# One transformer block with a mixture of experts on one Trainium2 core: the second parts of the experts' weights move from two engines to one

## The chip, the core and the metric

The kernel runs as one program on one core of a Trainium2 chip. The core has a matrix engine (TensorE, PE in the profile; its weight loads are shown as PEld), a vector engine (VectorE, DVE), a scalar engine (ScalarE, ACT), a general-purpose engine (GpSimd, POOL) and a queue engine that issues most DMAs (SyncE, SP). Each engine runs its own list of instructions in order; an instruction waits on semaphores until what it needs is there. The metric is the device time of one execution, in microseconds; lower is better. Before the change it was 3081.26 us as the median of three runs, 3079.08 to 3086.68 us.

## The reference, cut to what matters

One layer of an encoder over 2048 tokens of width 1024: a mixer (differential attention beside a gated delta rule), then a mixture of experts. All inputs and outputs are float32. Only the last part matters here:

```python
def hier_moe(h, w_group, b_group, w_router, b_router, w1, w3, w2):
    ...                      # a token picks 1 of 4 groups, then 2 of the group's 8 experts
    def run(args):
        xblk, e = args       # a block of up to 128 tokens of expert e
        hid = jax.nn.silu(xblk @ w1[e]) * (xblk @ w3[e])
        return hid @ w2[e]
    yb = lax.map(run, (xb, blk_expert)).reshape(cap, D) * buf_w[:, None].astype(t.dtype)
    y = jnp.zeros((N, D), t.dtype).at[buf_tok].add(yb)
```

There are 32 experts; w1 and w3 are 1024 x 512 and w2 is 512 x 1024, so an expert has 6.3 MB of weights.

## The kernel before

The program has five phases, one after the other: the input projection, attention and the delta rule, the merge with the output projection, the routing, and the experts (`phase5`). The experts' stage is the last 900 us or so, and only it is touched.

**Two parts for every number.** PE multiplies in a shortened float format (fp32r). To keep float32's precision, a weight is split in two: a first part `hi`, a cast to the short format, and a second part `lo`, what the cast left out. A product x·w is made as three matmuls: x's first part with `hi` and with `lo`, and x's second part with `hi`.

**The work per expert.** `chunks` (L1546) loads an expert's weights as 12 tiles of 128 x 1024 float32, 512 KB each, on SP's queue, into a ring of 11 `raw` tiles (`NRAW`). `split` (L1561) takes the next loaded tile: ACT casts it to `hi` (L1568), another engine makes `lo` as raw minus hi (L1570), and SP issues one more load. `hi` and `lo` lie in rings of 12 tiles each (`NHI`, `NLO`), just one expert's worth; a tile of the next expert can be written only when the matmuls of the present one have read the tile in its place.

**Which engine makes `lo`.** `self.nsp` counts the splits. Of the first expert's twelve, numbers 2, 4 and 6 (`P0`) go to GpSimd, from the second expert on every fourth (`POOL`); the others go to DVE. That makes 96 on GpSimd and 288 on DVE. GpSimd also issues the gather of each block's tokens (L1579, L1637) and the scatter of its result (L1628, L1694) in this stage, in the same in-order list.

**A block.** The experts come in a fixed order by load rank (`ORDER`); an expert has one to three blocks, 46 in all: 34 full ones of 128 tokens (`block`, L1576) and 12 half ones of up to 64 (`half`, L1630). A full block gathers its tokens, transposes them on PE (`tx`, L1586), splits them (ACT `xh`, DVE `xl`, L1589), makes the products with w1 and w3 (`pa`, `pb`, L1597 and L1599: 48 matmuls), the gating (ACT L1605, DVE `hd` L1606 and L1607), a transpose and split of that (`th`, `dh`, `dl`), and the products with w2 (`py`, L1623 and L1624: 24 matmuls). A half block has 32 and 16 matmuls and a few more small DVE steps (`ha`, `hb`, L1667 to L1670). In an expert's last block, `split` is called between the matmuls, twelve times in all, for the next expert's tiles.

**What sets the order.** `pipeline` (L61) runs several blocks at once, each in a later step than the next. Within this, a scheduler in the framework places the instructions in each engine's list by its own estimate of when each will be ready, so a block's matmuls, another's transposes and a third's w2 products are interleaved on PE.

Of the kernel before, what the change touches and what calls it, by code (L numbers as in the profile page):

```python
# [9 lines left out]
F32 = mybir.dt.float32  # L10
# [4 lines left out]
ALU = mybir.AluOpType  # L15
# [21 lines left out]
NLO, NHI, NRAW, POOL = 12, 12, 11, 4  # L37
OHA, P0, KW, EB = (3,), (2, 4, 6), 7, 1
SPL = {0: 4, 2: 4, 3: 4}
NBLK = NEXP + N2 + N3  # L40
# [3 lines left out]
# gates of the last slab that wait for the attention, and the units of it that they come before  # L44
# [16 lines left out]
def pipeline(units, old_first=False):  # L61
    """each turn starts a unit and runs the older ones to their next "yield 1"; "yield 0" lets the others in between"""
# [19 lines left out]
class K:  # L82
# [59 lines left out]
    # ---------------------------------------------------------------- phase 1  # L142
    def phase1(self, late):
# [13 lines left out]
        with ExitStack() as ctx:  # L157
# [25 lines left out]
            def load_x(p):  # L183
                """two tiles of x, normalized"""
# [7 lines left out]
                # the second pair is waited for: its first tile by itself  # L192
# [100 lines left out]
            # per-partition gain of q: both maps' 64 channels  # L293
# [7 lines left out]
            # a head's scores are in units of its slope, a power of two, until the bias is on  # L301
# [254 lines left out]
    def gates_and_gdn(self, ctx, sm, ps, hxp, hh, hl):  # L556
# [33 lines left out]
        # softplus(x) = max(x, 0) + log1p(e), e = exp(-|x|); log1p(e) = ln(u) e / (u - 1), u = 1 + e  # L590
# [96 lines left out]
        def scan(t):  # L687
# [6 lines left out]
            for b in range(4):  # L694
                pb, o = slice(32 * b, 32 * b + 32), 32 * (b % 2)
                nc.sync.dma_start(T[pb, :, o:o + 32], TB[t, :, b].rearrange("h r c -> r h c"))
                nc.sync.dma_start(U[pb, :, o:o + 32], UB[t, :, b].rearrange("h r c -> r h c"))
                # the zero quarter of each pair of blocks
                G.memset((U if b % 2 else T)[pb, :, 32 - o:64 - o], 0.0)
# [11 lines left out]
            # inverse of the unit triangular matrix, block doubling 32 -> 64 -> 128  # L711
# [32 lines left out]
            # recurrence over tiles of 128 tokens  # L744
# [76 lines left out]
    # ---------------------------------------------------------------- branch merge  # L821
    def merge_setup(self, ctx, ps):
# [6 lines left out]
        def load_o(s, n, h):  # L829
            """a head's output of a slab, as parts"""  # L830
# [54 lines left out]
    # ---------------------------------------------------------------- phase 2  # L885
    def phase2(self, cm, late):
# [3 lines left out]
        with ExitStack() as ctx:  # L890
# [8 lines left out]
            # ---- constants  # L899
# [16 lines left out]
            # distances of keys from queries, the last chunk's first half of queries doesn't see its second half of keys  # L916
# [9 lines left out]
            # ---- attention  # L926
            kv, qs = {}, {}

            def kv_tiles(p, h, n):
                """the first 512 keys' tiles come last: their memory is free first"""  # L930
# [6 lines left out]
            def kv_load(p, h, n):  # L937
                """the keys and values of a head, n chunks"""
# [11 lines left out]
            def q_load(h, s):  # L950
# [7 lines left out]
                # numerators, their first maps' sums and sums of squares, of four query tiles  # L958
# [6 lines left out]
            def att(p, h, qt, sp_pool, w):  # L965
# [47 lines left out]
                # out = o / l1, rms-normalised; a mean square beyond float32 gives 0, as its rsqrt does  # L1013
# [27 lines left out]
            def units():  # L1041
# [14 lines left out]
                for i, (p, h, qt) in enumerate(todo):  # L1056
                    wn = TS * (p + 2)
                    if wn != w:
# [4 lines left out]
                        # the first pass's lies where the merge's tiles come, which are not to be loaded before  # L1063
# [31 lines left out]
    # ---------------------------------------------------------------- phase 3  # L1095
    def phase3(self, cm):
# [5 lines left out]
        with ExitStack() as ctx:  # L1102
# [72 lines left out]
            def outp(i, s, j):  # L1175
# [29 lines left out]
                # logits of a slab by columns: 36 rows of the weights' first parts, 36 of their second  # L1205
# [44 lines left out]
    # ---------------------------------------------------------------- phase 4  # L1250
    def route_consts(self, ctx):
# [3 lines left out]
        # descending weights 8..1, expert number, iota over slots columns and partitions  # L1255
# [14 lines left out]
        # an expert's share of the schedule, in half blocks: one, and one more for each of these its rank lies below  # L1270
# [3 lines left out]
        self.nsp = 0  # L1274
# [13 lines left out]
    def first(self, sm, x, n, tg):  # L1288
        """one-hot of the first maximum over the last axis of x, and the maximum"""
# [16 lines left out]
    def route_a(self, sm, t0, t1):  # L1306
        nc = self.nc
        V, A = nc.vector, nc.scalar
        n = t1 - t0
# [10 lines left out]
        # the two best experts of every group  # L1320
# [13 lines left out]
        # their weights  # L1334
# [10 lines left out]
    def route_b(self, c, sm, wk, wp, ps):  # L1345
# [8 lines left out]
        # loads of the experts, as a column and in every row  # L1354
# [6 lines left out]
        # positions of the assignments within their experts  # L1361
# [4 lines left out]
        # rank of an expert: experts in falling order of load, ties in expert order  # L1366
# [9 lines left out]
        # expert of a rank  # L1376
# [8 lines left out]
        # the schedule: NBLK blocks in rank order, what goes beyond an expert's share after them  # L1385
# [12 lines left out]
        # base, share and first further block of an expert in one number  # L1398
# [37 lines left out]
        # token and weight of a slot; the weight in two parts  # L1436
# [26 lines left out]
        # the other experts' weights are read after the first rows  # L1463
# [11 lines left out]
        # blocks beyond the schedule: how many, and each expert's range of them  # L1475
# [6 lines left out]
        def weights():  # L1482
# [5 lines left out]
            # halved, for the tanh form of silu  # L1488
# [5 lines left out]
    def spots(self, wk, wp, g, act=False):  # L1494
        """one-hot rows of the places in their blocks, of eight tiles of assignments"""
# [16 lines left out]
    def rows_of(self, pool, pt, nm):  # L1512
        """rows to gather and to add to, from a table of token numbers counted from 1, 0 where there is none"""
# [11 lines left out]
    # ---------------------------------------------------------------- phase 5  # L1525
    def phase5(self):
# [3 lines left out]
        with ExitStack() as ctx:  # L1530
# [15 lines left out]
            def chunks(e, i):  # L1546
                """loads of an expert's weights, two rows of 128 of w1 and w3 or one of w2 at a time"""
# [13 lines left out]
            def split(more):  # L1561
                """the next loaded weights' parts, and another load"""
# [236 lines left out]
```

## Time and profile before

| | |
|---|---|
| median of three runs | 3081.26 us |
| the profiled execution | span 3079.4 us from its first to its last instruction; the page lists no other time of it, and the median of the runs is 1.9 us above this span |
| mean granted TensorE clock | 0.966 |
| first DVE split, last result row scaled | 2171.1 us, 3066.3 us |
| PE's first matmul on a second part (`pa` of a half block) | 2180.6 us |
| DMA in the whole program | 561.20 MB |

A row of a grouped view reads: source line, engine, operation, what is written and read, shapes, count | busy us, mean ns of one | idle us of the engine before them, and who ended that idleness. A row of the timeline reads: start, length, engine, line, operation, how many were merged, and in brackets the idle time before it and its releaser. PE's matmuls overlap each other: one lasts 0.39 us, the next starts 0.23 us after it.

### The profile page before, as it was taken

Reading aid. Unit: us, or ns where it says so; the run is one execution under the profiler, and the core shown is the slowest. Engines: PE = TensorE matmul, PEld = TensorE weight load, DVE = VectorE, ACT = ScalarE, POOL = GpSimd, SP = SyncE. Lnnn points to the kernel's source line nnn. Section 1 sums busy time; section 2 is a strip of 40 time slices with the busy share of each in tenths; the row PEclk is TensorE's granted clock in tenths of the full one; section 3 lists DMA queues with packets and bytes.
Section 4 is the critical chain, followed back from the end, with each engine's and each line's share of the span. In section 5 each row is a group of like instructions: output and inputs, shape, how many; then the busy total and the mean of one; then the engine's idle time right before and its main releaser. Section 6 shows DMA issues by size and latency. Waiting matters only on the chain. (4 is left out here: it accounts for less than half of the span.)

```text
span 3079.4 us, 43963 instructions
## 1 busy us (share of the span) xinstructions
PE 2844.8 (92%) x14845; PEld 2294.6 (75%) x14845; DVE 2079.0 (68%) x4804; ACT 1332.7 (43%) x2409; POOL 837.8 (27%) x614
## 2 busy tenths in 40 slices
PE   6999999999999999999899999997799899999897
PEld 4888778777877777777788787786577677667675
DVE  7567669985276443377757655676867767886876
ACT  4512223333322333377555543221545545554554
POOL 2200000000221222001342324221544545543553
PEclk9999999999999999999999999998799999999998
DMA  6334652221554664585676647532978888886895
GB/s 224 119 86 117 202 182 80 79 67 53 165 144 130 185 179 147 149 200 148 167 179 171 168 110 235 195 144 103 324 240 259 260 258 292 294 291 217 271 312 148
DMA packets 426245, 561.20 MB, mean 182 GB/s; under 512 B 56520, under 2 KB 240920, under 8 KB 426016
## 3 DMA queue, kind: packets, MB, share of 16 engines
q1 hardware_dynamic: 340560, 440.87, 46.4%
q10 hardware_dynamic: 73744, 75.53, 7.3%
q0 software_dynamic: 11712, 41.95, 5.8%
q8 instruction: 119, 1.95, 0.3%
q14 instruction: 110, 0.90, 0.1%
HBM read 436.06 MB, written 122.18 MB: 181 GB/s over the span
## 5 line engine op out<-in xcount | busy, mean ns | idle before, releaser
L1570 DVE TENSOR_TENSOR low<-raww,hiw 128x1024 fp32r<-128x1024 f32 x288 | 434.4, 1554 | 46.8 <-ACT hiw L1568 44.2
L1568 ACT CAST hiw<-raww 128x1024 fp32r<-128x1024 f32 x384 | 378.8, 1048 | 153.6 <-PE py L1624 67.7
L1570 POOL TENSOR_TENSOR low<-raww,hiw 128x1024 fp32r<-128x1024 f32 x96 | 263.2, 2771 | 118.9 <-ACT hiw L1568 112.7
L982 DVE CUSTOM_DVE_ANT_0 sp<-sc,M 128x512 f32<-128x512 f32 (+1 forms) x320 | 183.6, 604 | 53.1 <-PE sc L980 52.0
L548 PE MATMUL pg<-hh,ghi 128*128 128x512 f32 x512 | 210.5, 411 | 2.5 <-ACT ghi L539 2.5
L332 PE MATMUL mma<-whi,hh 128*128 128x512 f32 x512 | 208.5, 407 | 2.4 <-ACT hh L248 1.0
L550 PE MATMUL pg<-hh,glo 128*128 128x512 f32 x512 | 208.3, 407 | 0.0
L549 PE MATMUL pg<-hl,ghi 128*128 128x512 f32 x512 | 208.0, 406 | 0.0
L334 PE MATMUL mma<-whi,hl 128*128 128x512 f32 x512 | 202.8, 396 | 0.6 <-DVE hl L249 0.6
L333 PE MATMUL mma<-wlo,hh 128*128 128x512 f32 x512 | 202.1, 395 | 0.4 <-DVE wlo L255 0.4
L987 ACT ACTIVATE sp<-sp,mx 128x128 f32<-128x128 f32 (+15 forms) x128 | 153.7, 1201 | 46.4 <-DVE mx L985 40.7
L1006 PEld LDWEIGHTS av<-V,aT 128*128 128x128 f32 x1088 | 140.2, 196 | 34.6 <-ACT aT L1004 26.7
L1006 PE MATMUL av<-V,aT 128*128 128x128 f32 x1088 | 151.6, 284 | 13.9 <-ACT aT L1004 12.7
L255 POOL TENSOR_TENSOR wlo<-raw,whi 128x512 fp32r<-128x512 f32 x12 | 16.9, 1428 | 533.0 <-ACT whi L254 533.0
L342 PE MATMUL mmb<-hh,whi 128*128 128x512 f32 x384 | 155.3, 404 | 5.4 <-ACT whi L254 5.4
L344 PE MATMUL mmb<-hh,wlo 128*128 128x512 f32 x384 | 151.1, 393 | 0.6 <-POOL wlo L255 0.4
L343 PE MATMUL mmb<-hl,whi 128*128 128x512 f32 x384 | 150.3, 391 | 0.0
L979 PE MATMUL sc<-K,qd 128*128 128x512 f32 (+1 forms) x320 | 132.1, 416 | 14.7 <-DVE mx L982 10.9
L1623 PE MATMUL py<-hiw,dh 128*128 128x512 f32 x272 | 115.1, 423 | 20.4 <-ACT dh L1614 20.3
L1597 PE MATMUL pb<-low,xh 128*128 128x512 f32 x272 | 112.7, 414 | 18.3 <-DVE low L1570 10.7
L1579 POOL DMA_INDIRECT x<-h,sgi x34 | 63.6, 1872 | 230.1 <-PE tx L1586 132.7
L1597 PE MATMUL pa<-low,xh 128*128 128x512 f32 x272 | 111.3, 409 | 11.9 <-DVE low L1570 11.9
(555 smaller groups left out, 7522.3 us busy)
## 6 DMA issues: line engine op xcount, KB each, us to landing
raww<-in_w_dram SPq DMA_DIRECT2D x384, 512.0 KB
mw<-in_w_ada_dram SPq DMA_DIRECT2D x64, 256.0 KB
gate<-gt ACTq DMA_DIRECT2D x64, 256.0 KB
g<-gate SPq DMA_DIRECT2D x64, 256.0 KB
graw<-in_w_in_dram SPq DMA_DIRECT2D x52, 256.0 KB
raw<-in_w_in_dram SPq DMA_DIRECT2D x22, 512.0 KB
K<-k_hi SPq DMA_DIRECT2D x36, 256.0 KB
K<-k_lo SPq DMA_DIRECT2D x36, 256.0 KB
```

The source lines that it names most:

```text
L332: nc.tensor.matmul(pt[:, :n], a, his[k][:, :n], start=(k == 0), stop=False)
L333: nc.tensor.matmul(pt[:, :n], a, los[k][:, :n], start=False, stop=False)
L334: nc.tensor.matmul(pt[:, :n], b, his[k][:, :n], start=False, stop=(k == KT - 1))
L342: nc.tensor.matmul(pt, a, hh[s][:, k, :], start=(k == 0), stop=False)
L548: nc.tensor.matmul(pt, hi[:, k, :], hh[:, k, :], start=(k == 0), stop=False)
L549: nc.tensor.matmul(pt, hi[:, k, :], hl[:, k, :], start=False, stop=False)
L550: nc.tensor.matmul(pt, lo[:, k, :], hh[:, k, :], start=False, stop=(k == KT - 1))
L982: V.tensor_tensor_reduce(out=b[:, k0:k0 + n], in0=pt[:, :n], in1=Mt[:, mo:mo + n], op0=ALU.add, op1=ALU.min, scale=SLOPES[h], scalar=3e38, ...
L1006: PE.matmul(av[:, :P], aT[:, k * P:(k + 1) * P], Vt[k4 // 4][:, k, :], start=(k4 + k == 0), stop=(k4 + k == qt))
L1568: A.copy(hi, raw)
L1570: on.tensor_tensor(out=lo, in0=raw, in1=hi.bitcast(F32), op=ALU.subtract)
L1597: PE.matmul(p_, xh[:, k, :], w[i, n, k][q], start=(k == 0 and q == 0), stop=False)
```

## The change

GpSimd no longer makes any second part; all 384 subtractions are on DVE. The two constants that chose the engine and the counter are gone. Comments are deleted all over the file as well, which moves the line numbers by 3 (L1570 of before is L1568 after, L1586 is L1583). The loads, the casts, the matmuls, the gathers and the scatters are the same in number and kind.

```diff
-NLO, NHI, NRAW, POOL = 12, 12, 11, 4
-OHA, P0, KW, EB = (3,), (2, 4, 6), 7, 1
+NLO, NHI, NRAW = 12, 12, 11
+OHA, KW, EB = (3,), 7, 1
...
-        self.nsp = 0
...
                 A.copy(hi, raw)
-                on = G if (self.nsp % POOL == POOL - 1 if i else self.nsp in P0) else V
-                on.tensor_tensor(out=lo, in0=raw, in1=hi.bitcast(F32), op=ALU.subtract)
-                self.nsp += 1
+                V.tensor_tensor(out=lo, in0=raw, in1=hi.bitcast(F32), op=ALU.subtract)
```

The scheduler makes new lists out of this. Three places follow; in a tile's name the first number is the expert's place in the order, the second the tile's own.

GpSimd's list early in the stage, before the change:

```order
L1570 TENSOR_TENSOR low_2_21691<-raww_2_21558,hiw_2_21690 128x1024
L1579 DMA x_21993<-h_18355,sgi 128x1024
L1570 TENSOR_TENSOR low_2_21827<-raww_2_21606,hiw_2_21826 128x1024
L1628 DMA out_dram<-yo_21780,ssi 2176x1024
L1570 TENSOR_TENSOR low_3_21899<-raww_3_21664,hiw_3_21898 128x1024
L1570 TENSOR_TENSOR low_3_21939<-raww_3_21803,hiw_3_21938 128x1024
L1637 DMA x_22181<-h_18355,sgi 64x1024
```

The same place after the change:

```order
L1576 DMA x_21993<-h_18355,sgi 128x1024
L1625 DMA out_dram<-yo_21780,ssi 2176x1024
L1634 DMA x_22181<-h_18355,sgi 64x1024
L1625 DMA out_dram<-yo_21963,ssi 2176x1024
L1576 DMA x_22316<-h_18355,sgi 128x1024
```

What moved: the four subtractions between the gathers and the scatters are gone from this list, and nothing stands in their place.

DVE's list where the tiles of the fourth expert in the order (`low_3`) are made, before the change; `ha`, `hb` and `xl` below are steps of a half block and of the block behind it:

```order
L1627 SCALAR_TENSOR_TENSOR yo_21780<-py_21795,wt,g_21029 128x512
L1589 TENSOR_TENSOR xl_21837<-tx_21845,xh_21836 128x512
L1570 TENSOR_TENSOR low_3_21863<-raww_3_21622,hiw_3_21862 128x1024
L1570 TENSOR_TENSOR low_3_21869<-raww_3_21640,hiw_3_21868 128x1024
L1570 TENSOR_TENSOR low_3_21893<-raww_3_21646,hiw_3_21892 128x1024
L1570 TENSOR_TENSOR low_3_21913<-raww_3_21670,hiw_3_21912 128x1024
L1570 TENSOR_TENSOR low_3_21919<-raww_3_21688,hiw_3_21918 128x1024
L1570 TENSOR_TENSOR low_3_21933<-raww_3_21694,hiw_3_21932 128x1024
L1667 TENSOR_TENSOR ha_21944<-ha_21944,pa_21852 64x512
L1667 TENSOR_TENSOR hb_21945<-hb_21945,pb_21853 64x512
L1589 TENSOR_TENSOR xl_21996<-tx_21997,xh_21995 128x512
```

The same place after the change, with one more row ahead of it:

```order
L1568 TENSOR_TENSOR low_2_21827<-raww_2_21606,hiw_2_21826 128x1024
L1624 SCALAR_TENSOR_TENSOR yo_21780<-py_21795,wt,g_21029 128x512
L1586 TENSOR_TENSOR xl_21837<-tx_21845,xh_21836 128x512
L1568 TENSOR_TENSOR low_3_21863<-raww_3_21622,hiw_3_21862 128x1024
L1568 TENSOR_TENSOR low_3_21869<-raww_3_21640,hiw_3_21868 128x1024
L1568 TENSOR_TENSOR low_3_21893<-raww_3_21646,hiw_3_21892 128x1024
L1568 TENSOR_TENSOR low_3_21899<-raww_3_21664,hiw_3_21898 128x1024
L1568 TENSOR_TENSOR low_3_21913<-raww_3_21670,hiw_3_21912 128x1024
L1568 TENSOR_TENSOR low_3_21919<-raww_3_21688,hiw_3_21918 128x1024
L1568 TENSOR_TENSOR low_3_21933<-raww_3_21694,hiw_3_21932 128x1024
L1568 TENSOR_TENSOR low_3_21939<-raww_3_21803,hiw_3_21938 128x1024
L1664 TENSOR_TENSOR ha_21944<-ha_21944,pa_21852 64x512
```

What moved: eight subtractions stand in a row ahead of `ha`, `hb` and `xl` where there were six, and one more (`low_2_21827`) stands ahead of the `yo` before them; the three are GpSimd's of the first fence.

PE's list at the second transposes of that same block (`tx_22004`, which write into a PSUM tile that `xl_21996` has to read first), before the change:

```order
L1597 MATMUL pa_22011<-low_3_21893,xh_21836 128x512
L1586 MATMUL tx_22004<-ident,x_21834 128x128 x4
L1597 MATMUL pb_22012<-hiw_3_21898,xh_21836 128x512
L1623 MATMUL py_21964<-hiw_2_21799,dh_21959 128x512
L1623 MATMUL py_21964<-low_2_21800,dh_21959 128x512
```

After the change, the end of the matmuls that now come first, with the same transposes behind them:

```order
L1594 MATMUL pb_22012<-hiw_3_21918,xh_21836 128x512
L1594 MATMUL pb_22012<-low_3_21919,xh_21836 128x512
L1596 MATMUL pa_22011<-hiw_3_21912,xl_21837 128x512
L1583 MATMUL tx_22004<-ident,x_21834 128x128 x4
L1620 MATMUL py_21964<-hiw_2_21799,dh_21959 128x512
L1620 MATMUL py_21964<-low_2_21800,dh_21959 128x512
```

What moved: between `pa` with `low_3_21893` and the transposes stand 15 matmuls of 128x512 that stood behind them before. In a like place of the sixth expert in the order, nine matmuls now stand ahead of the first `py` that stood behind its first four; elsewhere the two lists agree over long stretches.

## The prediction

> **What bounds the kernel now.** I read the page's engine totals first, then its costliest groups, then the windows of the experts' stage, then who PE waits for, and last the timeline at PE's longest stops. The two lists of the changed engines' work on the page:
>
> ```profile
> span 3079.4 us, 43963 instructions
> ...
> L1570 DVE TENSOR_TENSOR low<-raww,hiw 128x1024 fp32r<-128x1024 f32 x288 | 434.4, 1554 | 46.8 <-ACT hiw L1568 44.2
> ...
> L1570 POOL TENSOR_TENSOR low<-raww,hiw 128x1024 fp32r<-128x1024 f32 x96 | 263.2, 2771 | 118.9 <-ACT hiw L1568 112.7
> ```
>
> The reader sees 288 subtractions on DVE at a mean of 1554 ns and 96 on GpSimd at 2771 ns. The windows view of the stage, from PE's settled start to the last block's end (busy us of PE, PEld, DVE, ACT, POOL; granted clock; DMA share; GB/s):
>
> ```profile
> 2203.00:3067.00 864.00, 796.92 (x3512) 610.96 (x3511) 647.96 (x636) 466.29 (x587) 425.84 (x179) 0.96 0.81 264
> ```
>
> PE is busy 797 of 864 us, DVE 648: PE bounds the stage, and 67 us of it are PE's own idle time. The 0.96 is a second loss: 4% of 864 us, or 35 us, went in a slower clock. Who ended PE's idle time, in total us, times and longest, from the waits of PE from 2200 us on:
>
> ```profile
> PE py L1623 <- ACT dh L1614: 20.3, 9, 5.3
> PE tx L1586 <- DVE xl L1589: 15.5, 3, 5.2
> PE pa L1597 <- DVE low L1570: 11.9, 13, 2.2
> PE pb L1597 <- DVE low L1570: 10.7, 11, 2.6
> PE pb L1597 <- POOL low L1570: 7.6, 6, 5.0
> ```
>
> These five rows are 66 us, nearly all of it. Only the last names GpSimd; why the others matter to this change is in the single durations of one DVE subtraction (min/median/max ns), and of `yo`'s last step in half blocks, with that step's group:
>
> ```profile
> L1570 DVE TENSOR_TENSOR low<-raww,hiw x288: 1203/1214/5653, 2171.1 to 3051.8; 128x1024 fp32r<-128x1024 f32 x144
> L1692 DVE SCALAR_TENSOR_TENSOR yo<-yo,wt,g x24: 733/744/2966, 2211.1 to 3050.0; 64x512 f32<-64x512 f32 x24
> ...
> L1692 DVE SCALAR_TENSOR_TENSOR yo<-yo,wt,g 64x512 f32<-64x512 f32 x24 | 36.8, 1535 | 0.2
> ```
>
> Most take 1.21 us, a few up to 5.65. Against the medians DVE loses 288 x (1554 - 1214) = 98 us and 24 x (1535 - 744) = 19 us, together **117 us**. Where it goes shows at PE's longest kind of stop (DVE, then POOL, then PE, in the timeline):
>
> ```profile
> 2240.46 12.82 DVE L1570 TENSOR_TENSOR low<-raww,hiw 128x1024 fp32r<-128x1024 f32 x6
> 2254.41 0.67 DVE L1589 TENSOR_TENSOR xl<-tx,xh 128x512 fp32r<-128x512 f32 x1
> ...
> 2243.59 2.99 POOL L1570 TENSOR_TENSOR low<-raww,hiw 128x1024 fp32r<-128x1024 f32 x1
> 2246.76 3.17 POOL L1570 TENSOR_TENSOR low<-raww,hiw 128x1024 fp32r<-128x1024 f32 x1 [0.18 <-ACT hiw L1568]
> ...
> 2255.14 1.11 PE L1586 MATMUL tx<-ident,x 128*128 128x128 f32 x4 [5.19 <-DVE xl L1589]
> ```
>
> Six subtractions take 12.82 us on DVE while GpSimd makes two. Six undisturbed ones are this long (and PE stops briefly there too):
>
> ```profile
> 2356.57 6.88 DVE L1570 TENSOR_TENSOR low<-raww,hiw 128x1024 fp32r<-128x1024 f32 x6
> ...
> 2362.38 0.50 PE L1597 MATMUL pb<-low,xh 128*128 128x512 f32 x1 [0.40 <-DVE low L1570]
> ```
>
> So in a row one takes 6.88 / 6 = 1.15 us, and DVE lost 5.9 us to two subtractions of GpSimd, about their whole length: the two engines hardly make `lo` at once. DVE then reaches `ha`, `hb` and `xl` late, and PE waits.
>
> **The change part by part.** *Removed:* 96 subtractions on GpSimd, and with them DVE's 117 us. *Added:* 96 x 1.15 = 110 us on DVE. DVE's sum is therefore the same within 7 us, some 640 of 864 us; the gain is not less work but where it falls. I go by kinds of stop.
>
> *`xl`.* At 2240 us two parts come to DVE (2.3 us), and one more ahead of `yo` (1.15): 5.9 - 3.4 = 2.5 us of the 5.19 go, 48%; of 15.5 us, **7.5**.
>
> *`dh`.* The usual place, DVE and PE:
>
> ```profile
> 2318.13 7.49 DVE L1570 TENSOR_TENSOR low<-raww,hiw 128x1024 fp32r<-128x1024 f32 x3 [0.30 <-ACT hiw L1568]
> ...
> 2327.40 0.79 PE L1623 MATMUL py<-hiw,dh 128*128 128x512 f32 x1 [3.54 <-ACT dh L1614]
> ```
>
> Three subtractions lose 7.49 - 3.4 = 4.1 us; two parts come to DVE (2.3); 1.8 of 3.54 us go, half; of 20.3 us, **10.3**.
>
> *`low` behind DVE.* One of three like places:
>
> ```profile
> 2734.24 13.24 DVE L1570 TENSOR_TENSOR low<-raww,hiw 128x1024 fp32r<-128x1024 f32 x6
> ...
> 2743.10 0.50 PE L1597 MATMUL pa<-low,xh 128*128 128x512 f32 x1 [1.00 <-DVE low L1570]
> ...
> 2746.40 0.79 PE L1597 MATMUL pb<-low,xh 128*128 128x512 f32 x1 [2.57 <-DVE low L1570]
> ```
>
> Here 13.24 - 6.9 = 6.3 us are lost to three parts that cost 3.4 on DVE: 2.9 of the 3.57 us go, 81%. Of the 22.6 us I take out about 4 that belong to late loads (below), so **14** to 15; I take 14.
>
> *`low` behind GpSimd.* 7.6 us, 5.0 in one stop. A part on DVE takes 1.2 us instead of 2.8 and never stands behind a scatter: **5**.
>
> *Clock.* 35 us. The next two rows are a stop of 2.2 us and the stretch just after it:
>
> ```profile
> 2586.70:2589.00 2.30, 0.09 (x2) 0.06 (x1) 2.30 (x3) 1.04 (x1) 0.00 (x0) 1.00 1.10 310
> 2589.26:2592.67 3.41, 3.25 (x8) 2.11 (x7) 3.41 (x5) 2.26 (x4) 2.52 (x1) 0.50 1.05 329
> ```
>
> The clock was halved for 3.4 us after a stop of only 2.2. The stops above shrink to 2.7, 1.7 and 0.7 us, so many remain long enough. The ends are 0 and 35; I take a third, **11**.
>
> *Against it.* In bursts without collisions, as at 2356 us, GpSimd's two parts ran for free and DVE now has 2.3 us more ahead of a stop that exists already. I find three such bursts, and five with one part: between 0 (DVE idles there later) and 13 us; I take **8**, nearer the upper end because PE already waits there.
>
> *Scatters and gathers* stay on GpSimd with nothing between them. GpSimd's own waits for gathers are for a free buffer:
>
> ```profile
> POOL x L1579 <- PE tx L1586: 132.7, 20, 12.5
> ...
> PEld tx L1644 <- DMA x<-h,sgi: 7.7, 1, 7.7
> ```
>
> A gather is thus issued as soon as PE has read an older block's tokens, and PE waits for one only once, the stage's first; they cost nothing, and would only if their lead over PE were gone. *SP, ACT:* the loads and casts keep their order; a `raw` tile is free sooner, which can only help the loads.
>
> Sum: 7.5 + 10.3 + 14 + 5 + 11 - 8 = **40 us**. The profiled span is 3079.4 us and the median 1.9 above it, so 3081.3 - 40 = **3041 us**.
>
> **The rivals.**
>
> *Zero sum.* 117 us go, 110 come; if the wait only moves along DVE's list, the time stays within 9 us (0.3%, about what a measurement of this kernel tells from no change): 3081 less the 7 us of the sums, 3074. For it: DVE's list is in order and `xl`, `hd` and `yo` now stand behind more subtractions. Against: DVE has 216 idle us in the stage.
>
> *Loads.* The stage moves 864 us x 264 GB/s = 228 MB. The fastest long stretch, and casts that wait for a load:
>
> ```profile
> 2592.00:2660.00 68.00, 65.56 (x296) 50.80 (x295) 51.70 (x53) 39.36 (x48) 35.06 (x17) 1.00 0.95 331
> ...
> 2585.51 1.05 ACT L1568 CAST hiw<-raww 128x1024 fp32r<-128x1024 f32 x1 [1.82 <-DMA raww<-in_w_dram]
> ...
> ACT hiw L1568 <- DMA raww<-in_w_dram: 8.4, 8, 2.4
> ```
>
> At 331 GB/s the 228 MB need 689 us, so the whole is not bound by them; but where experts of one block follow each other the share is already 0.95, and PE can't go faster there. If half of the gain falls in such stretches, 20 us are left: 3061.
>
> *A better plan.* PE's new list has 15 matmuls (15 x 0.234 = 3.5 us) ahead of the `tx` that waits, more than the 2.7 us that I left, and nine (2.1 us) ahead of a `py` against 1.8. If that holds throughout, the rest of `xl` and `dh` (18 us) and half of the clock (12) go too: 70 us, 3011.
>
> *The clock comes back whole.* If the shortened stops no longer halve the clock, the term is 35 instead of 11: 3017. For it: the two windows are one pair, and the 5.19 and 3.54 us stops are the common ones. Against it: in that pair 2.2 us were enough. The Trainium skill, "TensorE: Matmul & The Clock Gate", section "What's actually happening", says that the clock falls to half after an idle window of about 3.4 us, which would be this rival; the quoted pair speaks against the rule.
>
> *Slower.* DVE becomes the bound in last blocks: twelve parts are 13.8 us, beside 4 to 6 us of a block's own steps, against 12 us of matmuls in a half block. If only the bursts at PE's some 15 longer stops count as lost time (5.4 us each, the mean of the three quoted, 81 us) but all 110 added us are in PE's way, the time grows by 29 us to 3110. It decides by whether DVE's idle time lies in the blocks that get the parts. The Trainium skill, "Perfetto Trace Analysis", section "Optimizing Scalar/DVE Operations", says that where DVE is saturated, moving work to GpSimd may make sense, though it might not help since the two share a read port: undoing that would cost time if DVE were full. At 648 of 864 us the trace does not show it full.
>
> **How the numbers follow.** Chances: forecast 0.38 (3041, some 15 either way), loads 0.16 (3061), a better plan 0.13 (3011), the clock 0.05 (3017), zero sum 0.12 (3074), slower 0.16 (3110). The first four are faster by over 0.3%: 0.72; the same 0.12; slower 0.16. The range takes in the clock's case, the better plan (2999 with all of the clock, which I cut to 3002), the zero sum, and the milder half of the slower case, up to 3092; about 0.15 is left outside.
>
> **What would show it.** In the changed kernel's profile: 384 DVE subtractions with mean near the 1214 ns median and no maximum above 1.5 us; no `low` on POOL; DVE busy near 640 us in the stage; PE's waits for `dh` and `xl` halved, for POOL `low` gone; a mean clock in the stage near 0.97. Wrong would be: DVE subtractions still over 1.5 us on average (the loss was not GpSimd's); PE waiting as long in total but for DVE `low` (zero sum or slower); or `hiw` waiting for loads by tens of us.

## The result: 2996 us, and where PE's stops went

The changed kernel takes 2996.28 us (median of four runs, 2989.41 to 3000.1), the kernel before 3083.97 us beside it (3079.08 to 3087.09): 0.9719 of its time, with a 95% interval of 0.9703 to 0.9734, or some 87 us less. The direction was forecast, the size wasn't: 3041 us, and 3002 at the low end of the range.

All of it lies in the experts' stage. Its start can be read off the last matmuls ahead of it, `ptab`; first the kernel before, then the changed one (the operation's durations, then its first and last start, from a tile's view):

```profile
L1460 PE MATMUL ptab<-oc,oh x32: 376/387/407, 2161.8 to 2170.0; 128*128 128x46 f32 x32
```

```profile
span 2997.3 us, 43960 instructions
...
L1459 PE MATMUL ptab<-oc,oh x32: 377/387/405, 2164.4 to 2172.7; 128*128 128x46 f32 x32
```

From there to the end of the span it was 3079.4 - 2161.8 = 917.6 us, and is 2997.3 - 2164.4 = 832.9: **85 us less**. What lies ahead of it is the same work. Its length scatters: among the runs below `ptab` starts between 2148 and 2164 us where nothing ahead of it was changed, so stages are compared, not the ends of two profiles.

The groups of the page and a tile's view show DVE without collisions:

```profile
L1568 DVE TENSOR_TENSOR low<-raww,hiw 128x1024 fp32r<-128x1024 f32 x384 | 445.9, 1215 | 21.3 <-ACT hiw L1567 20.6
```

```profile
L1568 DVE TENSOR_TENSOR low<-raww,hiw x384: 1204/1215/1232, 2173.7 to 2969.4; 128x1024 fp32r<-128x1024 f32 x192
```

The mean is the median, and the longest of 384 took 1.23 us where it had been 5.65. DVE's sum is 446 us in place of 434: as forecast, the gain isn't less work for DVE. The windows view of the stage (busy us of PE, PEld, DVE, ACT, POOL; clock; DMA share; GB/s) and PE's waits in it:

```profile
2205.00:2985.00 780.00, 762.06 (x3497) 590.19 (x3495) 639.13 (x729) 462.46 (x585) 164.26 (x88) 1.00 0.89 292
```

```profile
PE py L1620 <- ACT dh L1611: 10.1, 9, 1.8
PE pa L1594 <- DVE low L1568: 4.9, 5, 3.6
PE py L1621 <- DVE dl L1612: 1.2, 1, 1.2
PE tx L1583 <- DVE xl L1586: 0.8, 1, 0.8
PE pb L1594 <- DVE low L1568: 0.4, 1, 0.4
```

PE's idle time went from 67 us to 18, its waits from 66 to 17, and the clock from 0.96 to 1.00. Its busy time fell from 797 to 762 us on the same matmuls but for 15 that the window doesn't show (some 3.5 us), since fewer of them ran at half clock. DMA carries 292 GB/s at a share of 0.89, and ACT's casts wait 0.7 us for a load in the whole stage: the loads were not the limit.

One long stop is left. The timeline shows DVE, then PE:

```profile
2428.07 8.02 DVE L1568 TENSOR_TENSOR low<-raww,hiw 128x1024 fp32r<-128x1024 f32 x7
...
2433.88 0.50 PE L1594 MATMUL pa<-low,xh 128*128 128x512 f32 x1 [3.61 <-DVE low L1568]
```

DVE's row counts the parts that start before the view's end at 2435 us. PE goes on at 2433.88 us, 5.81 us after the row's start: that is about five parts of 1.15 us, so it needs the row's fifth part and simply arrives before it is made, behind the small steps that end a half block.

### The profile page after: what moved, and what is told of

Its sections match the earlier page's. It is cut to its first block, busy times and chain, and to the rows that moved or that the text cites. A ratio compares the mean times of both kernels' runs of the same rounds, so it can differ in the third digit from the quotient of the medians.

```text
span 2997.3 us, 43960 instructions
## 1 busy us (share of the span) xinstructions
PE 2815.3 (94%) x14845; PEld 2276.4 (76%) x14845; DVE 2068.7 (69%) x4900; ACT 1331.4 (44%) x2409; POOL 567.2 (19%) x518
## 3 DMA queue, kind: packets, MB, share of 16 engines
q8 instruction: 119, 1.95, 0.3%
## 5 line engine op out<-in xcount | busy, mean ns | idle before, releaser
L1568 DVE TENSOR_TENSOR low<-raww,hiw 128x1024 fp32r<-128x1024 f32 x384 | 445.9, 1215 | 21.3 <-ACT hiw L1567 20.6
L1006 PEld LDWEIGHTS av<-V,aT 128*128 128x128 f32 x1088 | 138.9, 194 | 33.6 <-ACT aT L1004 25.5
L1576 POOL DMA_INDIRECT x<-h,sgi x34 | 73.1, 2150 | 360.9 <-PE tx L1583 204.0
L980 PE MATMUL sc<-K,ql 128*128 128x512 f32 (+1 forms) x320 | 119.6, 381 | 2.0 <-DMA ql<-q_lo 2.0
L1620 PE MATMUL py<-hiw,dh 128*128 128x512 f32 x272 | 109.9, 404 | 10.3 <-ACT dh L1611 10.1
L332 PEld LDWEIGHTS mma<-whi,hh 128*128 128x128 f32 x512 | 97.0, 189 | 25.2 <-ACT hh L248 1.7
L334 PEld LDWEIGHTS mma<-whi,hl 128*128 128x128 f32 x512 | 96.9, 189 | 23.0 <-DVE hl L249 1.7
```

Of the source, the lines that this page charges most:

```text
L332: nc.tensor.matmul(pt[:, :n], a, his[k][:, :n], start=(k == 0), stop=False)
L334: nc.tensor.matmul(pt[:, :n], b, his[k][:, :n], start=False, stop=(k == KT - 1))
L1006: PE.matmul(av[:, :P], aT[:, k * P:(k + 1) * P], Vt[k4 // 4][:, k, :], start=(k4 + k == 0), stop=(k4 + k == qt))
L1568: V.tensor_tensor(out=lo, in0=raw, in1=hi.bitcast(F32), op=ALU.subtract)
```

## The experiments

Three explanations were open: the end of the collisions between DVE and GpSimd (theory C); the new order of PE's list, which the scheduler made (rival O); and DVE's time as such, its own or stretched (theory D). In the diffs below, `hold_pe(ORDER)` stands for a few lines that tie each of PE's instructions of the stage, by a table, behind its predecessor in the list named; it adds no wait for data. The diffs also leave out the setting up of counters and scratch tiles. Holding a list costs nothing by itself: in the run stops (below), which holds the changed kernel's own list, 819.0 us lie between the first `ptab` and the last `yo` of a full block, in the changed kernel 819.5 us.

| run | what | us | of the kernel before | 95% interval |
|---|---|---|---|---|
| oldorder | changed kernel, PE's list of before | 3034.2 | 0.9837 | 0.9821 to 0.9853 |
| neworder | kernel before, PE's list of the changed one | 3084.4 | 1.0004 | 0.9990 to 1.0019 |
| pool2 | changed, useless subtractions on GpSimd | 3123.3 | 1.0132 | 1.0116 to 1.0149 |
| dve2 | changed, the same on DVE | 3085.9 | 1.0005 | 0.9990 to 1.0021 |
| dve2_free | dve2, PE's list not held | 3068.4 | 0.9970 | 0.9952 to 0.9987 |
| dve1 | half of dve2's | 3034.8 | 0.9861 | 0.9835 to 0.9886 |
| pool1 | changed, useless copies on GpSimd | 3008.5 | 0.9769 | 0.9739 to 0.9799 |
| dose48 | kernel before, 48 parts on GpSimd for 96 | 3026.5 | 0.9838 | 0.9817 to 0.9860 |
| slackorder | changed, PE's list of dve2_free | 2995.1 | 0.9740 | 0.9717 to 0.9764 |
| tx_old | changed, second transposes as early as before | 3014.7 | 0.9797 | 0.9778 to 0.9816 |
| tx_new | oldorder, second transposes as late as after | 3038.0 | 0.9885 | 0.9863 to 0.9906 |
| after_again | changed kernel | 2988.7 | 0.9726 | 0.9708 to 0.9744 |
| merge_dve, merge_dve5 | changed, the merge's parts on DVE too | 2984.9, 2980.9 | 0.9684, 0.9684 | 0.9656 to 0.9712, 0.9663 to 0.9704 |

Differences in us below are differences of these ratios times 3084, unless they are of stages.

### PE's list against the collisions

oldorder keeps all parts on DVE and takes PE's order from before:

```diff
             pipeline(units())
+            hold_pe(ORDER_OF_BEFORE)
```

> All 384 subtractions on DVE as after the change, but PE's list in the experts' stage is held to that of before the change, instruction by instruction. Theory C (the end of the collisions between DVE and GpSimd is the whole gain, PE's list matters little): within 10 us of the changed kernel's 2996, so 2990 to 3006. Rival O (PE's new list, with more matmuls ahead of those that wait, made the stops shrink beyond my forecast): the stops that I had left for xl and dh come back, 18 us, and half of the clock's loss, 14 us or so: 3020 to 3035, with PE's waits for dh and xl at 25 us or more.

It took 3034 us, at the upper end of rival O's range, with PE's waits for `dh` and `xl` at 22 us where O expected 25. The move to DVE alone, with PE's list as it was, is worth 0.0163, or **50 us** (43 by the stage, below); the new list is worth 0.0118, **36 us** more. PE's waits and the stage in this run:

```profile
span 3032.9 us, 43970 instructions
...
L1532 PE MATMUL ptab<-oc,oh x32: 376/387/406, 2158.6 to 2166.9; 128*128 128x46 f32 x32
```

```profile
2200.00:3020.00 820.00, 777.51 (x3505) 596.37 (x3505) 638.65 (x726) 464.94 (x586) 163.37 (x87) 0.99 0.84 277
```

```profile
PE py L1693 <- ACT dh L1684: 14.2, 9, 2.8
PE tx L1656 <- DVE xl L1659: 8.0, 3, 2.7
PE pa L1667 <- DVE low L1641: 7.2, 6, 1.9
PE py L1694 <- DVE dl L1685: 4.8, 8, 0.9
PE py L1756 <- DVE dh L1748: 2.4, 9, 0.4
PE tx L1656 <- DVE dh L1748: 2.0, 1, 2.0
PE pb L1667 <- DVE low L1641: 2.0, 5, 0.4
```

The stage is 3032.9 - 2158.6 = 874.3 us. From before to oldorder PE's idle time fell by 67.1 - 42.5 = 24.6 us and its busy time by 19.4; from oldorder to the changed kernel by 24.5 and 15.4. So both steps are half stops and half clock (the windows differ by seven and eight matmuls, some 2 us each).

The place that the prediction worked through shows both steps. Before, PE stopped there for 5.19 us. In oldorder, DVE and PE:

```profile
2235.98 9.16 DVE L1641 TENSOR_TENSOR low<-raww,hiw 128x1024 fp32r<-128x1024 f32 x8
2246.25 0.68 DVE L1659 TENSOR_TENSOR xl<-tx,xh 128x512 fp32r<-128x512 f32 x1
...
2246.99 0.66 PE L1656 MATMUL tx<-ident,x 128*128 128x128 f32 x4 [2.71 <-DVE xl L1659]
```

In the changed kernel:

```profile
2238.93 9.16 DVE L1568 TENSOR_TENSOR low<-raww,hiw 128x1024 fp32r<-128x1024 f32 x8
2249.21 0.68 DVE L1586 TENSOR_TENSOR xl<-tx,xh 128x512 fp32r<-128x512 f32 x1
...
2250.61 0.60 PE L1583 MATMUL tx<-ident,x 128*128 128x128 f32 x4
```

DVE does the same in both, eight parts in 9.16 us and then `xl`. In oldorder PE stands for 2.71 us; in the changed kernel no bracket stands behind the transposes: other matmuls come first, and `xl` is done when PE gets there.

neworder is the converse, the kernel before with PE's new list:

```diff
             pipeline(units())
+            hold_pe(ORDER_OF_AFTER)
```

> The subtractions on both engines as before the change (96 on GpSimd), but PE's list is held to that of the changed kernel. Theory C: as before the change within 15 us, 3069 to 3099, DVE's subtractions still at a mean of about 1.55 us. Rival O: PE's better list hides a good part even with the collisions, 3030 to 3055.

3084 us, no change: theory C's figure. The new list is worth nothing while GpSimd still makes parts:

```profile
PE pb L1670 <- POOL low L1643: 25.5, 13, 3.1
PE pa L1670 <- DVE low L1643: 17.9, 9, 4.8
```

PE now waits 25.5 us for GpSimd's parts, where it was 7.6: it comes to them at a place that fits a DVE part. So the two gains aren't independent; the list's 36 us need GpSimd's parts gone.

The two lists differ more than the three places shown ahead of the prediction tell: of PE's 3609 instructions that the tables hold, 460 have to be moved to make one list of the other, and the second group of transposes stands elsewhere in 32 of the 46 blocks. To see which part of the list counts, the second group of a block's transposes was put back to its old distance behind the first in the new list (tx_old), and to its new distance in the old list (tx_new). Counted in the lists with 0.23 us for a matmul, the mean distance over the 46 blocks is 5.6 us of work before and 7.0 after.

```diff
             pipeline(units())
+            hold_pe(ORDER_OF_AFTER, second_tx_as_in=ORDER_OF_BEFORE)
```

> The changed kernel with its own PE list, except that the second group of a block's transposes stands as early behind the first as before the change (counted in PE instructions between them; 32 of 46 blocks differ). Theory X (the later place of instructions that wait for DVE, these transposes above all, is what PE's new list is worth): 18 to 30 of the 38 us are lost, 3014 to 3026, with the waits of tx for xl at 8 us. Rival Y (the place of the w2 products behind th and of the products with late second parts counts, not that of the transposes): within 8 us of 2996.

```diff
-            hold_pe(ORDER_OF_BEFORE)
+            hold_pe(ORDER_OF_BEFORE, second_tx_as_in=ORDER_OF_AFTER)
```

> The run with PE's list held to that of before (3034 us), except that the second group of transposes stands as late as in the changed kernel's list. Theory X: 18 to 30 us less, 3004 to 3016. Rival Y: 3026 to 3036. In between, 8 to 18 us less, both places count.

> The changed kernel once more, beside the two above on one chip and for the comparison with the version that has the merge's second parts on DVE too (0.9684, 0.9663 to 0.9704): 0.9705 to 0.9735 of the kernel before if that version is really faster, 0.966 to 0.970 if not.

tx_old lost 0.9797 - 0.9726 = 0.0071, 22 us (25 by the stage): theory X's range. PE's waits there:

```profile
PE tx L1657 <- DVE xl L1660: 11.1, 9, 2.7
...
PE tx L1657 <- DVE dl L1686: 5.5, 3, 1.8
```

tx_new, the converse, won nothing, against theory X: by the ratio it lost 0.0048, 15 us, against oldorder, by the stage of the profiled execution 3 us. PE no longer waits for `xl` there, but for `dh` instead, 23.8 us for 14.2:

```profile
PE py L1693 <- ACT dh L1684: 23.8, 12, 2.6
```

So the late place of the transposes is needed, but isn't enough. The w2 products stand as far behind the transposes ahead of them (`th`) in tx_new as in oldorder, in every block: 2.4 us of PE's work on average, where the changed kernel's list has 3.2 and tx_old 3.3. What PE no longer waits for at the transposes it then waits for at the w2 products. The rest of the new list without the late transposes (tx_old against oldorder) is worth 0.0040, 12 us, the transposes on top of it 22, the transposes alone nothing: the list works as a whole. The w2 products by themselves weren't tried.

slackorder tries another list on the changed kernel, made for more DVE work:

```diff
             pipeline(units())
+            hold_pe(ORDER_OF_DVE2_FREE)
```

> The changed kernel, no useless work in it, but PE's list is the one that the scheduler made for the kernel with 106 us more work on DVE: matmuls that wait for DVE stand later. Theory F with a gain left: PE's remaining stops of 17 us shrink, 2980 to 2994. Rival (the list of the changed kernel fits already, and a later place only moves other work): 2996 to 3020.

0.9740, with an interval that overlaps the changed kernel's, and 5 us longer by the stage: nothing to be had that way, against theory F.

### What a microsecond on DVE costs

pool2 puts the collisions back without GpSimd's results being needed; dve2 puts the same useless work on DVE itself. PE's list is held to that of the changed kernel.

```diff
                 V.tensor_tensor(out=lo, in0=raw, in1=hi.bitcast(F32), op=ALU.subtract)
+                if count % 4 == 3 if i else count in (2, 4, 6):
+                    for z in (slice(0, 448), slice(448, 896)):
+                        junk = wk.tile([P, 448], F32R, tag="junk", bufs=1)
+                        G.tensor_tensor(out=junk, in0=raw[:, z], in1=hi[:, z].bitcast(F32), op=ALU.subtract)  # dve2: V
+                count += 1
```

> The changed kernel with PE's list held, and beside it useless work on GpSimd: at the same 96 splits that it made before, GpSimd makes two subtractions of 128x448 from the same two tiles into a scratch tile that nobody reads. Nobody waits for GpSimd's results, DVE makes all 384 parts itself. Theory C: DVE's subtractions are stretched again by 100 us or more in sum and the time goes back by 60 to 130 us, to 3055 to 3125. Rival (what hurt was waiting for GpSimd's own results and its late scatters and gathers, not DVE's stretching): no more than 10 us, 2996 to 3006.

> The changed kernel with PE's list held, and the same useless subtractions (two of 128x448 at 96 splits) on DVE itself: some 96 x 1.1 = 106 us more DVE work, without collisions. Theory D (DVE time is DVE time: stretched by GpSimd or its own, it delays the same): the time grows as much as with the useless work on GpSimd, to 3055 or more. Theory C (a stretch costs more than own work, for it falls in bursts and in front of steps PE waits for, while own work is spread over DVE's 150 idle us): 3005 to 3030, clearly less than with the work on GpSimd.

The groups of pool2, then those of dve2:

```profile
L1641 DVE TENSOR_TENSOR low<-raww,hiw 128x1024 fp32r<-128x1024 f32 x384 | 554.3, 1497 | 22.9 <-ACT hiw L1640 21.5 <-DMA raww<-in_w_dram 0.8 <-PE pa L1732 0.4
L1645 POOL TENSOR_TENSOR junkw<-raww,hiw 128x448 fp32r<-128x448 f32 x192 | 383.7, 1998 | 116.9 <-ACT hiw L1640 52.8 <-issue 52.3 <-POOL junkw L1645 2.4
```

```profile
L1641 DVE TENSOR_TENSOR low<-raww,hiw 128x1024 fp32r<-128x1024 f32 x384 | 448.9, 1216 | 19.4 <-ACT hiw L1640 18.5 <-DMA raww<-in_w_dram 0.5 <-PE pa L1732 0.4
L1645 DVE TENSOR_TENSOR junkw<-raww,hiw 128x448 fp32r<-128x448 f32 x192 | 118.1, 615 | 0.1
```

In pool2 `low` lost 554 - 446 = 108 us to GpSimd's work, and the kernel became 127 us slower. PE never waits for that work; ACT does for 13 us in two places, and its casts wait 4 us for loads, so what is left is the stretching of DVE, as theory C has it. Two more of DVE's steps were stretched, the last ones of `yo` (27.3 us for 17.7 in dve2) and of `ha` (20.3 for 16.3); both read two operands from SBUF, as `low` does. Steps that read one of theirs from PSUM lost nothing: `xl` took 45.8 us for 45.9. In all DVE lost some 122 us. In dve2 118 us of own work cost 88 us, where C expected 9 to 34. So C is wrong in holding that own work on DVE is nearly free, and D in holding that both cost the same: a stretched microsecond cost 127/122 = 1.04, an own one 88/118 = **0.75**. dve1 makes half the own work:

```diff
-                if count % 4 == 3 if i else count in (2, 4, 6):
+                if count % 8 == 7 if i else count == 2:
```

> The changed kernel with PE's list held and the useless subtractions on DVE at half as many splits (every eighth, one of the first expert's twelve): some 58 us more DVE work, where 118 us cost 90. If every microsecond of own work costs the same (0.76): 44 us, 3035 to 3045. If DVE has some slack that is filled first: 10 to 25 us, 3006 to 3021.

44 us for half of 118, 0.74 again: there is no slack that fills first. dve2_free asks whether a list that knows of the work does better:

```diff
             pipeline(units())
-            hold_pe(ORDER_OF_AFTER)
```

> The same as the run with 106 us of useless subtractions on DVE, which took 3086 us, but PE's list isn't held: the scheduler places PE's matmuls knowing of the added DVE work. Theory F (what costs is that DVE's real times differ from those that PE's list was made for): much of the 90 us goes, 3010 to 3045. Rival W (DVE's work itself is in the way in the experts' last blocks, whatever PE's order): 3065 to 3090.

0.9970 for 1.0005, so 11 us of 88 come back (17 by the stage): rival W. PE waits for `low` there:

```profile
PE pa L1599 <- DVE low L1568: 31.7, 14, 5.1
```

A fitting list is worth something here too, but the work itself is in the way. dose48 has half of the collisions, with the scheduler free:

```diff
-NLO, NHI, NRAW, POOL = 12, 12, 11, 4
-OHA, P0, KW, EB = (3,), (2, 4, 6), 7, 1
+NLO, NHI, NRAW, POOL = 12, 12, 11, 8
+OHA, P0, KW, EB = (3,), (2,), 7, 1
```

> The kernel before with half as many subtractions on GpSimd: every eighth from the second expert on and one of the first expert's twelve, 47 or 48 in all. If every collision costs the same, the time lies half way, 3030 to 3050. If a few collisions already spoil PE's list (theory F): above the middle, 3055 to 3080. If only bursts in which two of GpSimd's parts fall together hurt: 3000 to 3025. DVE's subtractions lose about half of the 98 us in each case.

The median is a little under the range for equal costs, the ratio in it: the first half of the parts taken from GpSimd brought 0.0162, 50 us, the second half 0.0119, 37 us. With an interval of 6 to 7 us to either side the two halves can't be told apart, so equal costs aren't refuted; nor are they shown, for each step has a new list of the scheduler's in it. DVE's `low` lost 336 x (1335 - 1214) = 41 of the 98 us there, about half, as expected.

pool1 asks what of GpSimd's work collides:

```diff
-                        G.tensor_tensor(out=junk, in0=raw[:, z], in1=hi[:, z].bitcast(F32), op=ALU.subtract)
+                        G.tensor_copy(junk.bitcast(F32), raw[:, z])
```

> As the run with useless subtractions on GpSimd (3123 us, DVE's subtractions at a mean of 1497 ns), but GpSimd only copies: two copies of 128x448 from the raw tile to the scratch tile at the same 96 splits, one operand read from SBUF in place of two. If any access of GpSimd to SBUF excludes DVE: again 3090 to 3125, mean of DVE's subtractions 1.4 us or more. If only an instruction of GpSimd that reads two operands does: 2996 to 3010 and a mean of 1.22 us.

A tile's view of the two (min/median/max ns):

```profile
L1641 DVE TENSOR_TENSOR low<-raww,hiw x384: 1203/1217/1947, 2169.3 to 2985.1; 128x1024 fp32r<-128x1024 f32 x192
```

```profile
L1645 POOL COPY junkw<-raww x192: 554/632/10122, 2156.9 to 2974.4; 128x448 f32<-128x448 f32 x192
```

Between the two expectations: 0.9769, some 15 us (20 by the stage), with a mean of 1275 ns for DVE's subtractions. A copy delays DVE too: the longest subtraction took 1.95 us, 0.73 more than the median, a little more than one copy. But a copy is short, and GpSimd's idle time ahead of the copies mostly ended with the load (283.5 us), so they mostly run before DVE comes; else it is the copy that waits, up to 10.1 us. The longest, at 2453 us, stands beside a row of eight subtractions of 9.16 us. The Trainium skill, "SBUF — State Buffer", section "Who interferes with whom", says that an instruction of DVE with two inputs from SBUF contends with one of GpSimd that reads SBUF, and that the ports they share are an exclusive lock; these rows agree.

### The clock

stops adds bursts of 60 matmuls with graded pauses behind the last block:

```diff
+            for j, width in enumerate([64, 192, 320, 448, 640, 832, 1024, 1280, 1536, 2048, 3072, 0, 0]):
+                for m in range(60):
+                    PE.matmul(pt, lhs[:, 0:128], rhs[:, 0:512], start=(m == 0), stop=(m == 59))
+                A.copy(lhs[:, 0:64], pt[:, 0:64])
+                for c0 in range(0, width, 512):
+                    A.copy(other[:, 0:min(512, width - c0)], pt[:, 0:min(512, width - c0)])
+                A.copy(lhs[:, 64:128], pt[:, 64:128])
```

> The changed kernel with PE's list held, and after its last block thirteen bursts of 60 matmuls of 128x512 on scratch data, with stops between them that ACT's copies of growing width set (about 1 to 5 us), so its time is some 250 us longer and isn't compared. Theory S (a stop of about 2 us is enough): stops up to 1.8 us leave the matmuls after them at 0.23 us apart, stops from 2.2 us on are followed by some 3 us of matmuls at twice that. Rival L (it takes about 3.4 us of idle time): stops of 2.2 to 3.2 us halve nothing. Rival G (it hangs on where the stop falls in a fixed grid of time): stops of 1.9 to 2.9 us halve it in some cases and not in others, all from 3.5 us on do.

The timeline's rows of four bursts (start, length, and in the bracket the stop ahead):

```profile
3083.62 14.26 PE L1817 MATMUL pt<-hitail,dhtail 128*128 128x512 f32 x60 [1.52 <-ACT dhtail L1822]
3099.80 15.81 PE L1817 MATMUL pt<-hitail,dhtail 128*128 128x512 f32 x60 [1.93 <-ACT dhtail L1822]
3117.75 14.27 PE L1817 MATMUL pt<-hitail,dhtail 128*128 128x512 f32 x60 [2.14 <-ACT dhtail L1822]
3134.77 15.70 PE L1817 MATMUL pt<-hitail,dhtail 128*128 128x512 f32 x60 [2.76 <-ACT dhtail L1822]
```

The windows view of the first microseconds of the last two (the last numbers are the clock, DMA's share and GB/s):

```profile
3117.75:3124.00 6.25, 6.25 (x27) 5.05 (x28) 0.00 (x0) 0.00 (x0) 0.00 (x0) 1.00 0.00 0
3134.77:3138.00 3.23, 3.23 (x8) 2.56 (x9) 0.00 (x0) 0.00 (x0) 0.00 (x0) 0.51 0.03 5
```

A burst takes 14.27 us, or some 1.5 us more when its start is halved. The stop of 1.93 us halved it and the longer one of 2.14 us didn't, so, against theory S, no length by itself is the threshold. The stop of 2.76 us halved it too, against rival L. Rival G is left: it hangs on where the stop falls. Of the other stops, those of 0.4 to 1.4 us halved nothing, and the one of 3.99 us did (15.80 us). It is one execution with one stop of each length; that the grid of time is a fixed one isn't shown by it. The Trainium skill, "TensorE: Matmul & The Clock Gate", section "What's actually happening", says that activity is watched in a window of 3.4 us that runs freely, which agrees with this; that an idle window of about 3.4 us is needed doesn't: 1.93 us were enough.

### The same change in another stage

merge_dve moves the merge's second parts of weights as well:

```diff
-                G.tensor_tensor(out=lo, in0=raw, in1=hi.bitcast(F32), op=ALU.subtract)
+                V.tensor_tensor(out=lo, in0=raw, in1=hi.bitcast(F32), op=ALU.subtract)
```

> The same kind of change in another stage, on top of the changed kernel: the 64 second parts of the merge's weights (128x512 each, 1.29 us undisturbed on GpSimd, 89 us in sum) go to DVE as well. DVE there loses only about 12 us to them, and would get 64 x 0.62 = 40 us of its own. By what the runs so far gave (a stretched us costs 1.08, an own us 0.6 to 0.76): 24 to 30 less 13, so 11 to 17 us slower than the changed kernel, 3005 to 3015. Rival (taking GpSimd's two-input instructions away always pays): 2980 to 2994. Rival (DVE is 62% busy there, PE 94%, so it has room): within 5 us of 2996.

> The same kernel as the run with the merge's second parts on DVE, which gave 0.9684 of the kernel before, 0.9656 to 0.9712 from three runs, where the changed kernel had 0.9719, 0.9703 to 0.9734; more rounds, to see whether it is faster than the changed kernel. The profiled executions reach the same instruction ahead of the experts' stage anywhere from 2148 to 2164 us without any change ahead of it, so one execution can't tell 10 us. If the gain of 10 us is real: 0.9665 to 0.9705 with the interval below 0.9715. If it is scatter: 0.9705 to 0.9730. If it is slower, as worked out from the price of own work: 0.975.

Both gave 0.9684. Beside the changed kernel's two figures, 0.9719 and 0.9726, this is some 12 us faster; against after_again the intervals of the longer run don't overlap, against the first measurement they touch (0.9703 and 0.9704). after_again lies where it was expected if that version is really faster. It is the fastest version of the study. The expectation worked out from DVE's price, 11 to 17 us slower, was wrong. The groups of this stage in the changed kernel, then in merge_dve5:

```profile
L847 POOL TENSOR_TENSOR wlw_branch_b<-rww_branch_b,whw_branch_b 128x512 fp32r<-128x512 f32 x32 | 44.9, 1402 | 196.7 <-ACT whw_branch_b L846 150.4 <-ACT ob L1008 30.7 <-DMA K<-k_hi 8.8
L847 POOL TENSOR_TENSOR wlw_branch_a<-rww_branch_a,whw_branch_a 128x512 fp32r<-128x512 f32 x32 | 44.6, 1393 | 48.2 <-ACT whw_branch_a L846 41.4 <-PE y L869 3.0 <-DMA mg<-g 2.4
```

```profile
L847 DVE TENSOR_TENSOR wlw_branch_a<-rww_branch_a,whw_branch_a 128x512 fp32r<-128x512 f32 x32 | 23.3, 728 | 1.7 <-ACT whw_branch_a L846 1.7
L847 DVE TENSOR_TENSOR wlw_branch_b<-rww_branch_b,whw_branch_b 128x512 fp32r<-128x512 f32 x32 | 22.7, 710 | 11.3 <-ACT whw_branch_b L846 11.2
```

No cost of DVE's 46 us of own work shows there, so the price of 0.75 belongs to the experts' stage, not to DVE as such. Why it gains stays open. The experts' stage is no shorter in these two runs (834.2 and 835.4 us from `ptab` on), so the gain lies ahead of it, and the way up to `ptab` scatters by more than the 12 us where nothing on it was changed (2148 to 2164 us).

## Why the prediction was wrong in size, step by step

**What bounds it, and the mechanism**: right. PE bounds the stage, DVE's 117 us were GpSimd's doing (all of them went; pool2 brings them back), DVE's sum stayed the same, and the gain came from PE's stops and the clock.

**The step that failed** is that each stop was worked out with PE's list as it stood, and that the sum took this for the whole. "A better plan" had the right mechanism, but as a rival at 0.13, for it rested on two places of the new list and I took the rest to be alike, where 460 of 3609 instructions had moved. The runs show 36 us there (41 by the stage). With the old list the sum holds: 43 us by the stage, 50 by the ratio, for the 40 forecast. That it comes this near is in part luck: the stops gave 4 us less than forecast and the clock 8 more.

**The terms, against oldorder**, where only they act: `xl` 15.5 - 8.0 = 7.5 us (forecast 7.5; at its own place 2.71 us were left of 5.19, forecast 2.7). `low` behind DVE 22.6 - 9.2 = 13.4 (14). `low` behind GpSimd 7.6 (5). `dh` 20.3 - 14.2 = 6.1 (10.3). The cost: new waits for `dl` and for a half block's `dh`, 4.8 + 2.4 + 2.0 = 9.2 (8), which are other stops than the ones at `low` that I had priced. Together 25 us of stops for the 29 forecast. One reading was loose: at 2240 us the end of a third subtraction of GpSimd (2239.00 to 2241.56 us) lies beside DVE's six as well, so DVE's 5.9 us were lost to some 7.3 us of GpSimd's work, not to 6.2.

**The clock** was the mis-sized term: 11 us forecast, and 19 us of PE's busy time went with the old list, 35 with the new one. I argued from one pair in which a stop of 2.2 us had halved the clock, and took two thirds to stay lost. Stops of 1.9 to 2.8 us do so only in some cases, and the one of 1.5 didn't; with the new list all of PE's waits but one are 1.8 us or shorter.

**The rivals.** Zero sum: wrong in the sum's consequence, as DVE's busy time as such isn't the measure, though with a grain of truth that I hadn't priced: own work isn't free but costs 0.75 us a us (dve2, dve1). Removing 117 stretched us at 1.04 and adding 110 at 0.75 gives 39 us, near the 43 to 50 that oldorder shows, though both prices were measured with the new list. Loads: wrong, 292 GB/s at a share of 0.89 were reached over the whole stage. Slower: wrong, no kind of stop grew by more than 1.2 us in sum. The clock whole: it came back, but together with the better plan, a case that I priced at 2999 and cut off at 3002.

**Gathers and scatters** cost PE nothing, as forecast, though some take far longer (below).

## What to carry to other kernels

A subtraction on GpSimd that excludes DVE isn't parallel work: price it by what DVE loses, and look for the loss as the gap between mean and median of DVE's own instruction. Where a scheduler makes the lists, a change of engine changes the list of the engine that waits, and that list must be compared over its whole length, not at two places: here it was worth nearly as much as the change itself, and nothing without it. The same kind of change paid again in a stage where the price worked out from this one said that it wouldn't, so a price holds for its stage.

## What else the runs showed of the hardware

Some of GpSimd's gathers and scatters take about as long as the rows of subtractions that DVE makes beside them. The changed kernel, a gather and a half block's scatter (min/median/max ns):

```profile
L1576 POOL DMA_INDIRECT x<-h,sgi x34: 936/1462/8758, 2176.2 to 2913.6; - x34
```

```profile
L1691 POOL DMA_INDIRECT out_dram<-yo,ssi x12: 1466/1566/10125, 2225.0 to 2967.5; - x12
```

The longest scatter, 10.12 us, began at 2447.49 us; DVE made eight subtractions beside it, from 2447.14 us on, in 9.16 us. The longest gather, 8.76 us at 2215.93 us, stands beside a subtraction, a step of `yo` and then six subtractions of 6.88 us. DVE's own rows aren't longer there. Before the change it was so too: the six undisturbed subtractions at 2356 us that the prediction shows have a scatter of 7.86 us beside them. PE waited for none of these here.
